# A hybrid decoder layer: the last gate summed at half the pace, weight sums in pairs, outputs of Down gated earlier, and an accumulator of its own for the last columns

## The chip, the cores and the metric

One core of a Trainium2 chip runs the whole layer in one launch. The metric is the device time of the core in microseconds; the time before is the median of three runs. All arithmetic is float32; the matmuls take each operand in two parts (a rounded high part and the rest), so that one product is three matmuls.

## The reference

For 512 tokens of width 1024 the layer computes a modulated norm, a mixture of two kinds of heads, and then a gated MLP. The change touches the MLP and the gate behind it alone:

```
h2 = rmsnorm(x, norm2_g[l]) * (1.0 + sc2) + sh2
u = causal_dwconv(h2 @ w_up[l], conv_w[l], conv_b[l])
a, v = jnp.split(u, 2, axis=-1)
x = x + gt2 * ((jax.nn.silu(a) * v) @ w_down[l])
```

`gt2` is the last sixth of `silu(c) @ w_ada + b_ada`, a vector of 1024. `w_up` is 1024 x 5632, `w_down` 2816 x 1024.

## The kernel before, in words

The order of the instructions on each engine is the order in which the program writes them. SP issues the plain loads and stores, POOL the accumulating ones, and a queue does not go past an instruction that waits.

**Up.** There are 44 steps (`st`), two for each of 22 column blocks of 128: one for the half `a`, one for the half `v`. `up_mm(st)` (L1713) issues 24 matmuls of 512 columns (three for each of 8 row blocks) into one accumulator. `next_parts` gets the weights of the step after: SP loads a block of 1 MB as `raw` (L206; two transfers, two buffers), ACT casts half of it to `whi` (L144) and DVE subtracts to get `wlo` (L145). `up_post` (L1723) applies the convolution and the SiLU on ACT and DVE, and POOL multiplies the halves and forms sums and differences of the two halves of the tokens (L1738 to L1746); `put_by` (L1748) stores one set of them, `later`, in HBM.

**The gate.** `ada_last` (L1468) computes `gt2` for two halves of 512 columns. For each of 8 row blocks SP loads 256 KB of `w_ada` into `aw` (L1478), POOL multiplies by the column `cs` and adds to an accumulator (L1479, L1480). An advance of the generator does one row block; then one advance splits the sum into `rhi` and `rlo` (ACT L144, DVE L145), and one sums over the partitions with two matmuls against ones (L1487, L1488). The Up loop advances it at every step from 3 on, so that 20 advances fill steps 3 to 22.

**Weight sums.** Down multiplies 2 x 2 blocks in a scheme with seven products, and needs four sums of blocks of `w_down`. `weight_sums` (L1693) makes them in HBM, by copies of SP and accumulating transfers of POOL, all of 256 KB, in six stages two steps apart, for each of 11 blocks `j`: copies (L1699, L1700), adds (L1691), a copy (L1705), an add, a copy (L1709), an add. A copy waits for the adds of the stage before it.

**Down.** There are 22 rounds (`u`) in two phases of 11. In the first, four products for two token blocks `i` fill eight accumulators; they are combined into the five tiles `m1, u2, u3, b12, c22` on ACT and DVE. In the second, three products fill six accumulators. `dn_load(u)` issues the loads three rounds ahead (in the second phase also the stored `later` block, L1777); `dn_split(u)` casts and subtracts one round ahead. `late` (L1894) multiplies a finished tile by the gate and adds `x1` (L1876, L1877) during the second phase: `c22`, which is stored, and `u3`. The last two rounds are run product by product, so that outputs end one by one: `dn_out` (L1910) takes three DVE instructions of 512 columns for each of four outputs (L1912 to L1914), `dn_last` (L1917) two for the rows of `u3` (L1919, L1920), the last of them in two halves of 256 columns that share one accumulator.

Of the kernel before, what the change touches and what calls it, by code (L numbers as in the profile page):

```python
# [19 lines left out]
P = 128  # L20
T = 512
# [32 lines left out]
EARLY = 6  # L54
ADAS = (3, 4, 2)
# [48 lines left out]
def hybrid_layer_kernel(ctx: ExitStack, tc: tile.TileContext, d: dict, out: bass.AP, dbg=None):  # L104
# [1581 lines left out]
    wt1, wt4 = (hbm.tile([NU, P, 512], F32, name=n) for n in ("wt1", "wt4"))  # L1686
    wt23 = hbm.tile([NU, P, 2, 512], F32, name="wt23")
    b_ = [[wd_view[:, r:NFF:2, 512 * c:512 * c + 512] for c in range(2)] for r in range(2)]

    def add(o, w):  # L1690
        gp.dma_start(o, w, accum_op=ALU.add)  # L1691

    def weight_sums(st):  # L1693
        for off, n in ((0, 0), (2, 1), (4, 2), (6, 3), (8, 4), (10, 5)):
            j, r = divmod(st - 3 - off, 3)
            if r or not 0 <= j < NU:
                continue
            if n == 0:
                sp.dma_start(wt23[j, :, 1], b_[1][1][:, j])  # L1699
                sp.dma_start(wt1[j], b_[0][1][:, j])  # L1700
            elif n == 1:
                add(wt23[j, :, 1], b_[0][1][:, j])
                add(wt1[j], b_[0][0][:, j])
            elif n == 2:
                sp.dma_start(wt23[j, :, 0], wt23[j, :, 1])  # L1705
            elif n == 3:
                add(wt23[j, :, 0], b_[0][0][:, j])
            elif n == 4:
                sp.dma_start(wt4[j], wt23[j, :, 0])  # L1709
            else:  # L1710
                add(wt4[j], b_[1][0][:, j])
# [43 lines left out]
    wraw, wsp = {}, {}  # L1755
    turn = [0]

    def a_split(u, a):
# [33 lines left out]
    def dn_split(u):  # L1792
# [49 lines left out]
    for st in range(3, nst):  # L1842
# [7 lines left out]
        next(ada2, None)  # L1850
# [43 lines left out]
    def late(u):  # L1894
        if u - NU in (3, 4):
            i = u - NU - 3
            gated(c22, right, i, 2, 512)
            sp.dma_start(out_view[:, 2 + i, 512:1024], c22[:, i])
        if u - NU in (5, 6):
            gated(u3, left, u - NU - 5, 2, 0)  # L1900

    for u in range(NU, n - 2):
        ahead_of(u)
        late(u)
# [3 lines left out]
    ahead_of(n - 2)  # L1908

    def dn_out(m, i, base, g, row, col):  # L1910
        t = TMP([P, T])
        ve.tensor_tensor(t, accs[m, i], base[:, i], ALU.add)  # L1912
        ve.tensor_tensor(t, t, g, ALU.mult)
        ve.tensor_tensor(t, t, x1[row][:, col:col + 512], ALU.add)  # L1914
        sp.dma_start(out_view[:, row, col:col + 512], t)

    def dn_last(i, row, c0, c1):  # L1917
        t = TMP([P, T])[:, 0:c1 - c0]
        ve.tensor_tensor(t, accs[4, i][:, c0:c1], left[:, c0:c1], ALU.mult)  # L1919
        ve.tensor_tensor(t, t, u3[:, i, c0:c1], ALU.add)  # L1920
        sp.dma_start(out_view[:, row, c0:c1], t)

    for m, base, g, col in ((2, m1, left, 0), (3, b12, right, 512)):
        for i in range(2):
            for u in (n - 2, n - 1):
                dn_mm(u, m, i)
            dn_out(m, i, base, g, i, col)
    for u in (n - 2, n - 1):
# [40 lines left out]
```

## Time and profile before

| | |
|---|---|
| median of three runs | 688.0 us (687.71 to 689.7) |
| the profiled execution | 690.0 us |
| its span, first to last instruction | 688.2 us |
| TensorE busy | 669.7 us (97%) |
| VectorE (DVE), ScalarE (ACT), GpSimd (POOL) busy | 500.0, 353.5, 199.6 us |
| mean granted TensorE clock | 0.991 |
| HBM read, written | 123.29 MB, 29.50 MB |

A row of the timeline is: start in us from the span's start, duration, engine, line, operation, tile written and tiles read, shape, and in brackets how long the engine had been idle before it and what ended that. Matmuls overlap, so their pace is read from start to start. A row of waits is: who waited for whom, total us, times, the longest. Durations of one kind are in ns.

### The profile page before, as it was taken

Reading aid. Unit: us, or ns where it says so; the run is one execution under the profiler, and the core shown is the slowest. Engines: PE = TensorE matmul, PEld = TensorE weight load, DVE = VectorE, ACT = ScalarE, POOL = GpSimd, SP = SyncE. Lnnn points to the kernel's source line nnn. Section 1 sums busy time; section 2 is a strip of 40 time slices with the busy share of each in tenths; the row PEclk is TensorE's granted clock in tenths of the full one; section 3 lists DMA queues with packets and bytes.
Section 4 is the critical chain, followed back from the end, with each engine's and each line's share of the span. In section 5 each row is a group of like instructions: output and inputs, shape, how many; then the busy total and the mean of one; then the engine's idle time right before and its main releaser. Section 6 shows DMA issues by size and latency. Waiting matters only on the chain.

```text
span 688.2 us, 11140 instructions
## 1 busy us (share of the span) xinstructions
PE 669.7 (97%) x4147; PEld 552.5 (80%) x4148; DVE 500.0 (73%) x964; ACT 353.5 (51%) x657; POOL 199.6 (29%) x211
## 2 busy tenths in 40 slices
PE   8999999999999999999999999979999999999995
PEld 4778898688888888888988888758888888888884
DVE  5778988978899878788556665845545558566987
ACT  5755337746777776255534443333443336454550
POOL 1006120000010101100079958986455346000000
PEclk9999999999999999999999999989999999999998
DMA  9936363566314135142268989999999846975562
GB/s 340 411 126 214 97 222 118 193 201 201 92 34 157 60 121 187 62 127 92 62 175 239 229 190 257 249 218 248 256 288 250 195 125 217 357 255 179 185 261 92
DMA packets 102876, 130.44 MB, mean 190 GB/s; under 512 B 7116, under 2 KB 68389, under 8 KB 102823
## 3 DMA queue, kind: packets, MB, share of 16 engines
q1 hardware_dynamic: 96055, 117.09, 51.4%
q0 software_dynamic: 6336, 11.54, 10.6%
q10 hardware_dynamic: 432, 1.12, 0.4%
q8 instruction: 32, 0.52, 0.3%
q14 instruction: 21, 0.17, 0.1%
HBM read 123.29 MB, written 29.50 MB: 222 GB/s over the span
## 4 chain that ended last, share of the span: by engine, by line
PE 75%; DVE 11%; ACT 5%; DMA 3%; POOL 3%; issue 1%; SPq 1%; ACTq 0%; POOLq 0%; DVEq 0%
PE u L150 10%; PE u L148 10%; PE u L149 10%; PE dn L149 5%; PE dn L148 5%; PE dn L150 5%; PE accq L657 3%; DMA aw<-in_w_ada 2%; PE oh L148 2%; PE oh L149 2%; PE oh L150 2%; PE oT L1126 2%; PE F L1097 2%; PE pT L148 2%; PE pT L149 2%; PE pT L150 2%
## 5 line engine op out<-in xcount | busy, mean ns | idle before, releaser
L145 DVE TENSOR_TENSOR wlo<-raw,whi 128x1024 fp32r<-128x1024 f32 (+1 forms) x67 | 92.8, 1386 | 94.5 <-ACT whi L144 94.3
L150 PE MATMUL u<-h2h,wlo 128*128 128x512 f32 (+1 forms) x360 | 138.0, 383 | 0.8 <-DVE wlo L145 0.8
L148 PE MATMUL u<-h2h,whi 128*128 128x512 f32 (+1 forms) x360 | 137.8, 383 | 0.0
L149 PE MATMUL u<-h2l,whi 128*128 128x512 f32 (+1 forms) x360 | 137.6, 382 | 0.0
L144 ACT CAST whi<-raw 128x1024 fp32r<-128x1024 f32 (+1 forms) x67 | 68.7, 1027 | 78.2 <-PE u L149 70.2
L150 PEld LDWEIGHTS u<-h2h,wlo 128*128 128x128 f32 x360 | 68.2, 190 | 15.1 <-DVE wlo L145 2.2
L149 PEld LDWEIGHTS u<-h2l,whi 128*128 128x128 f32 x360 | 68.4, 190 | 13.2
L148 PEld LDWEIGHTS u<-h2h,whi 128*128 128x128 f32 x360 | 68.4, 190 | 12.7
L349 POOL TENSOR_TENSOR hrs<-hrs,mhalf 128x4 f32<-128x4 f32 (+2 forms) x16 | 18.6, 1173 | 90.7 <-DVE hrs L348 88.7
L1733 ACT ACTIVATE y<-y 128x512 f32<-128x512 f32 x22 | 13.9, 632 | 55.1 <-DVE y L1730 55.0
L144 ACT CAST whi<-wd 128x1024 fp32r<-128x1024 f32 x20 | 21.0, 1052 | 40.5 <-PE dn L150 34.0
L1064 ACT ACTIVATE pt<-pt,mx 128x128 f32<-128x128 f32 (+3 forms) x64 | 36.0, 564 | 9.2 <-DVE mx L1048 8.1
L145 DVE TENSOR_TENSOR wlo<-wd,whi 128x1024 fp32r<-128x1024 f32 x20 | 25.6, 1278 | 19.7 <-ACT whi L144 19.4
L148 PE MATMUL pT<-hT,whi 128*128 128x512 f32 x96 | 38.3, 399 | 0.0
L149 PE MATMUL pT<-hT,whi 128*128 128x512 f32 x96 | 37.6, 391 | 0.0
L150 PE MATMUL pT<-hT,wlo 128*128 128x512 f32 x96 | 37.5, 391 | 0.0
L1691 POOL DMA_DIRECT2D wt<-in_w_down x44 | 36.8, 984 | 0.0
L1729 DVE SCALAR_TENSOR_TENSOR y<-u,cv,y 128x511 f32<-128x511 f32 x44 | 32.6, 741 | 2.9 <-ACT y L1728 2.9
L149 PE MATMUL dn<-wlo,as 128*128 128x512 f32 x88 | 34.4, 390 | 0.1
L148 PE MATMUL dn<-whi,as 128*128 128x512 f32 x88 | 34.2, 389 | 0.0
L150 PE MATMUL dn<-whi,as 128*128 128x512 f32 x88 | 34.2, 389 | 0.0
L1730 DVE SCALAR_TENSOR_TENSOR y<-u,cv,y 128x510 f32<-128x510 f32 x44 | 32.9, 749 | 1.6
(355 smaller groups left out, 1617.1 us busy)
## 6 DMA issues: line engine op xcount, KB each, us to landing
raw<-in_w_up SPq DMA_DIRECT2D x44, 512.0 KB, 6.0
aw<-in_w_ada SPq DMA_DIRECT2D x24, 512.0 KB, 3.9
wt<-in_w_down POOLq DMA_DIRECT2D x44, 256.0 KB, 7.0
ada<-in_ada_first SPq DMA_DIRECT2D x16, 512.0 KB, 8.1
raw<-in_w_in SPq DMA_DIRECT2D x7, 1024.0 KB, 5.0
wt<-in_w_down SPq DMA_DIRECT2D x22, 256.0 KB, 6.8
wt<-wt SPq DMA_DIRECT2D x22, 256.0 KB, 5.4
wd<-in_w_down SPq DMA_DIRECT2D x11, 512.0 KB, 4.4
```

The lines of the kernel that those rows point to most:

```text
L144: sc.copy(hi, src)
L145: (eng or ve).tensor_tensor(lo, src, f32(hi), ALU.subtract)
L148: pe.matmul(o, ah, bh, start=start, stop=False, skip_group_check=True)
L149: pe.matmul(o, ah, bl, start=False, stop=False, skip_group_check=True)
L150: pe.matmul(o, al, bh, start=False, stop=stop, skip_group_check=True)
L349: gp.tensor_tensor(o, o, mhalf[:, 0:n], ALU.pow)
L657: pe.matmul(accq[i], h[:, e, i * P:(i + 1) * P], w[:, f], start=(k + e + f == 0), stop=(e == 1 and k == KT - 1), skip_group_check=True)
L1064: sc.activation(pt[:, sl], pt[:, sl], AF.Exp, bias=mx[:, e:e + 1], scale=-1.0, accum_out=su[:, h % 2, e:e + 1])
L1691: gp.dma_start(o, w, accum_op=ALU.add)
L1729: ve.scalar_tensor_tensor(y[:, 1:], u[:, :T - 1], cv[:, 44 + c:45 + c], y[:, 1:], ALU.mult, ALU.add)
L1730: ve.scalar_tensor_tensor(y[:, 2:], u[:, :T - 2], cv[:, c:c + 1], y[:, 2:], ALU.mult, ALU.add)
L1733: sc.activation(y, y, AF.Silu)
```

## The change

1. The gate: the Up loop advances the generator at odd steps only, from step 3 to 41.
2. Weight sums: blocks `j` are taken in pairs (five pairs and a single one). The three sums that one pair needs lie in one tile `wt` of HBM, the fourth in `wt4`; each stage is one transfer for a pair (the first copies are two), so that a first add moves 1 MB. Stages start every six steps and stand two steps apart as before. POOL issues 18 adds where it issued 44, SP 24 copies where it issued 44. The products 6 and 7 of the first phase read their weights in the other order, to fit the new layout.
3. The second phase's first four `later` blocks are loaded (`back`) and split during rounds 5 to 9 of the first phase.
4. All of `c22, m1, u3, b12` get the gate and `x1` during the second phase; an output of the last rounds is then one multiplication by the gate and one addition.
5. The last 256 columns: the round before last is gated and added to `u3` early (`rest`). The weights of the last round's product 4 for those columns are multiplied by the gate and split again (`wgt`), and the product goes to an accumulator of its own, `dnt`; one addition to `rest` gives the output.

Cut to what is spoken of:

```diff
-    wt1, wt4 = (hbm.tile([NU, P, 512], F32, name=n) for n in ("wt1", "wt4"))
-    wt23 = hbm.tile([NU, P, 2, 512], F32, name="wt23")
+    groups = [range(j, min(j + 2, NU)) for j in range(0, NU, 2)]
+    wt = [hbm.tile([len(js), P, 3, 512], F32, name=f"wt{g}") for g, js in enumerate(groups)]
+    wt4 = [hbm.tile([len(js), P, 512], F32, name=f"wt4_{g}") for g, js in enumerate(groups)]
...
-            j, r = divmod(st - 3 - off, 3)
-            if r or not 0 <= j < NU:
+            g, r = divmod(st - 3 - off, 6)
+            if r or not 0 <= g < len(groups):
                 continue
+            js = groups[g]
+            rows = slice(2 * js[0], 2 * js[-1] + 2)
+            even, odd = (wd_view[:, rows][:, r::2] for r in range(2))
+            t, t4 = wt[g].rearrange("j p a c -> p j a c"), wt4[g].rearrange("j p c -> p j c")
             if n == 0:
-                sp.dma_start(wt23[j, :, 1], b_[1][1][:, j])
-                sp.dma_start(wt1[j], b_[0][1][:, j])
+                sp.dma_start(t[:, :, 0], even[:, :, 512:])
+                sp.dma_start(t[:, :, 1], odd[:, :, 512:])
             elif n == 1:
-                add(wt23[j, :, 1], b_[0][1][:, j])
-                add(wt1[j], b_[0][0][:, j])
+                gp.dma_start(t[:, :, 0:2], even.rearrange("p j (a c) -> p j a c", a=2), accum_op=ALU.add)
             elif n == 2:
-                sp.dma_start(wt23[j, :, 0], wt23[j, :, 1])
+                sp.dma_start(t[:, :, 2], t[:, :, 1])
             elif n == 3:
-                add(wt23[j, :, 0], b_[0][0][:, j])
+                gp.dma_start(t[:, :, 2], even[:, :, 0:512], accum_op=ALU.add)
...
         put_by(st - 4)
-        next(ada2, None)
+        if st % 2:
+            next(ada2, None)
...
         ahead_of(u)
+        if 0 <= u - EARLY + 1 < PRE:
+            back(u - EARLY + 1)
+        if 0 <= u - EARLY < PRE:
+            a_split(u - EARLY + NU, PB.pop(u - EARLY))
...
+    def late(v):
+        for t, i in [bases.pop(0) for _ in range((0, 1, 2, 2, 1, 1, 1, 0, 0)[v])]:
+            g, row, col = home[id(t)]
+            gated(t, g, i, row, col)
+            if t is c22:
+                sp.dma_start(out_view[:, row + i, col:col + 512], t[:, i])
...
+    def out_sum_of(acc, base, g):
+        t = TMP([P, T])[:, 0:acc.shape[1]]
+        ve.tensor_tensor(t, acc, g, ALU.mult)
+        ve.tensor_tensor(t, t, base, ALU.add)
+        return t
...
+    wgt = TMP([P, T], tag="wgt")[:, 0:256]
+    ve.tensor_tensor(wgt, w4raw[:, 256:512], left[:, 256:512], ALU.mult)
+    wgh, wgl = (G([256], F32R, s="wgt") for _ in range(2))
+    split(wgh, wgl, wgt)
+    both(2, 0)
+    dn_out(2, 0, m1, left, 0, 0)
...
+    dn_mm(n - 2, 4, 1)
+    rest = out_sum_of(accs[4, 1][:, 256:512], u3[:, 1, 256:512], left[:, 256:512])
...
+    dn_mm(n - 1, 4, 1, slice(0, 256))
+    dn_out(4, 1, u3, left, 3, 0, 256)
+    tail = PS("dnt")[:, 0:256]
+    ah, al = (z[:, P:2 * P] for z in AS[n - 1][TERMS[1][4][0]])
+    mm3(tail, ah, al, wgh, wgl, True, True)
+    t = TMP([P, T])[:, 0:256]
+    ve.tensor_tensor(t, tail, rest, ALU.add)
+    sp.dma_start(out_view[:, 3, 256:512], t)
```

How it moves instructions, at three places. First POOL in Up, before, from an add of weights on (`wt` the sums, `aw` the gate, `ga` and `gb` the products of the halves):

```order
L1691 DMA wt_3799<-in_w_down 128x512
L1691 DMA wt_3797<-in_w_down 128x512
L1479 TENSOR_TENSOR aw_4288<-aw_4288,cs 128x512
L1480 TENSOR_TENSOR aw_4288<-aw_4288 128x512
L1691 DMA wt_3799<-in_w_down 128x512
L1738 TENSOR_TENSOR gb_4453<-y_4496,y_4539 128x512
L1739 TENSOR_TENSOR ga_4452<-gb_4453 128x256
L1740 TENSOR_TENSOR ga_4452<-ga_4452 128x256
L1741 TENSOR_TENSOR gb_4453<-gb_4453,ga_4452 128x256
L1479 TENSOR_TENSOR aw_4288<-aw_4288,cs 128x512
L1480 TENSOR_TENSOR aw_4288<-aw_4288 128x512
L1479 TENSOR_TENSOR aw_4288<-aw_4288,cs 128x512
```

The same engine now, around the first add of the second pair:

```order
L1739 TENSOR_TENSOR gb_4453<-y_4494,y_4534 128x512
L1740 TENSOR_TENSOR ga_4452<-gb_4453 128x256
L1741 TENSOR_TENSOR ga_4452<-ga_4452 128x256
L1742 TENSOR_TENSOR gb_4453<-gb_4453,ga_4452 128x256
L1480 TENSOR_TENSOR aw_4297<-aw_4297,cs 128x512
L1481 TENSOR_TENSOR aw_4297<-aw_4297 128x512
L1704 DMA wt_3798<-in_w_down 128x2x1024
L1745 TENSOR_TENSOR ga_4617<-y_4574,y_4613 128x256
L1746 TENSOR_TENSOR gb_4618<-y_4574,y_4613 128x256
```

Between two sets of products stand one pair of gate instructions and one transfer; before, two pairs and one to three transfers.

Second SP in Up, before (`raw` is the next weights of Up):

```order
L206 DMA raw_4508<-in_w_up 128x8x128 x2
L1478 DMA aw_4288<-in_w_ada 128x512
L1705 DMA wt_3799<-wt_3799 128x512
L1478 DMA aw_4288<-in_w_ada 128x512
L1709 DMA wt_3798<-wt_3799 128x512
L206 DMA raw_4592<-in_w_up 128x8x128 x2
```

And now:

```order
L207 DMA raw_4503<-in_w_up 128x8x128 x2
L1479 DMA aw_4297<-in_w_ada 128x512
L1710 DMA wt_0_3803<-wt_3797 128x2x512
L207 DMA raw_4582<-in_w_up 128x8x128 x2
L1752 DMA later<-gb_4453 128x768
L1479 DMA aw_4297<-in_w_ada 128x512
L1706 DMA wt_3798<-wt_3798 128x2x512
L207 DMA raw_4667<-in_w_up 128x8x128 x2
```

A copy of a sum, which waits for an add, now stands right ahead of each load of Up's weights but every third, where two copies of 512 KB stand that wait for none.

Third the last instructions of DVE, before (`dn` are accumulators, `dc` the five tiles, `gt` the gate):

```order
L1912 TENSOR_TENSOR tmp_6834<-dn_6479,dc_6413 128x512
L1913 TENSOR_TENSOR tmp_6834<-tmp_6834,gt_3800 128x512
L1914 TENSOR_TENSOR tmp_6834<-tmp_6834,x_648_3499 128x512
L1919 TENSOR_TENSOR tmp_6845<-dn_6483,gt_3800 128x512
L1920 TENSOR_TENSOR tmp_6845<-tmp_6845,dc_6412 128x512
L1919 TENSOR_TENSOR tmp_6855<-dn_6487,gt_3800 128x256
L1920 TENSOR_TENSOR tmp_6855<-tmp_6855,dc_6412 128x256
L1919 TENSOR_TENSOR tmp_6862<-dn_6487,gt_3800 128x256
L1920 TENSOR_TENSOR tmp_6862<-tmp_6862,dc_6412 128x256
```

And now:

```order
L1927 TENSOR_TENSOR tmp_6798<-tmp_6798,dc_6390 128x512
L1926 TENSOR_TENSOR tmp_6805<-dn_6458,gt_3809 128x256
L1927 TENSOR_TENSOR tmp_6805<-tmp_6805,dc_6389 128x256
L1926 TENSOR_TENSOR tmp_6814<-dn_6450,gt_3809 128x512
L1927 TENSOR_TENSOR tmp_6814<-tmp_6814,dc_6390 128x512
L1926 TENSOR_TENSOR tmp_6824<-dn_6454,gt_3809 128x512
L1927 TENSOR_TENSOR tmp_6824<-tmp_6824,dc_6389 128x512
L1926 TENSOR_TENSOR tmp_6831<-dn_6458,gt_3809 128x256
L1927 TENSOR_TENSOR tmp_6831<-tmp_6831,dc_6389 128x256
L1960 TENSOR_TENSOR tmp_6839<-dnt_6835,tmp_6805 128x256
```

One addition stands behind the last product (`dnt`); `rest` (tmp_6805) has moved ahead of two outputs, and ahead of these rows stand the product and the subtraction of `wgt`.

More of the change, by code (lines that the diff above doesn't have):

```diff
@@ L54 @@
 EARLY = 6
+PRE = 4
 ADAS = (3, 4, 2)
@@ L1753, in put_by @@
                 a_split(j, PA.pop(j))
-    wraw, wsp = {}, {}
+    wraw, wsp, w4s = {}, {}, []
     turn = [0]
@@ L1762, in a_split, with back @@
         AS[u] = [(hi[:, q], lo[:, q]) for q in range(n)]
+    def back(j):
+        PB[j] = G([3, 256], s="gb")
+        sp.dma_start(PB[j], later[j])
     def dn_load(u):
@@ L1892, in hybrid_layer_kernel @@
                 ve.tensor_tensor(c22[:, i], o, u3[:, i], ALU.subtract)
[L1894 to L1900, printed above, removed]
+    bases = [(c22, 0), (c22, 1), (m1, 0), (m1, 1), (u3, 0), (u3, 1), (b12, 0), (b12, 1)]
+    home = {id(m1): (left, 0, 0), id(b12): (right, 0, 512), id(u3): (left, 2, 0), id(c22): (right, 2, 512)}
+    def late(v):
[4 more added lines that the diff above has]
+                sp.dma_start(out_view[:, row + i, col:col + 512], t[:, i])
     for u in range(NU, n - 2):
         ahead_of(u)
-        late(u)
+        late(u - NU)
         for m in TERMS[1]:
@@ L1908, in hybrid_layer_kernel @@
     ahead_of(n - 2)
[L1910 to L1928, printed above, removed]
-        dn_mm(u, 4, 0)
-    dn_last(0, 2, 0, 512)
-    dn_mm(n - 2, 4, 1)
-    for c in range(0, 512, 256):
-        dn_mm(n - 1, 4, 1, slice(c, c + 256))
-        dn_last(1, 3, c, c + 256)
+    w4raw = w4s[0][:, 0]
+    def out_sum_of(acc, base, g):
[3 more added lines that the diff above has]
+        return t
@@ new lines, in dn_out, with both @@
+    def dn_out(m, i, base, g, row, col, c1=512):
+        t = out_sum_of(accs[m, i][:, 0:c1], base[:, i, 0:c1], g[:, 0:c1])
+        sp.dma_start(out_view[:, row, col:col + c1], t)
+    def both(m, i):
+        for u in (n - 2, n - 1):
+            dn_mm(u, m, i)
+    wgt = TMP([P, T], tag="wgt")[:, 0:256]
[4 more added lines that the diff above has]
+    dn_out(2, 0, m1, left, 0, 0)
@@ new lines, in hybrid_layer_kernel @@
+    both(2, 1)
+    dn_out(2, 1, m1, left, 1, 0)
+    both(3, 0)
+    dn_out(3, 0, b12, right, 0, 512)
+    dn_mm(n - 2, 4, 1)
+    rest = out_sum_of(accs[4, 1][:, 256:512], u3[:, 1, 256:512], left[:, 256:512])
+    both(3, 1)
+    dn_out(3, 1, b12, right, 1, 512)
+    both(4, 0)
+    dn_out(4, 0, u3, left, 2, 0)
+    dn_mm(n - 1, 4, 1, slice(0, 256))
[3 more added lines that the diff above has]
+    mm3(tail, ah, al, wgh, wgl, True, True)
```

22 lines of the change are left out of this document (10 added, 12 removed).

## The prediction

> **What bounds the kernel now.** I read the page's first line and its busy times, then the stretches, then what PE waits for, and then the timeline where PE stood idle.
>
> ```profile
> span 688.2 us, 11140 instructions
> PE 669.7 (97%) x4147; PEld 552.5 (80%) x4148; DVE 500.0 (73%) x964; ACT 353.5 (51%) x657; POOL 199.6 (29%) x211
> ```
>
> TensorE is the bound: it is busy for all but 18.5 us. A gain here is an idle time of PE that goes, nothing else. Four stretches (PE, PEld, DVE, ACT, POOL busy with instructions, then granted clock, DMA share, GB/s):
>
> ```profile
> 360.00:400.00 40.00, 40.00 (x178) 33.10 (x177) 26.07 (x25) 17.27 (x22) 36.73 (x32) 1.00 0.89 220
> ...
> 440.00:480.00 40.00, 34.38 (x135) 26.81 (x135) 22.36 (x22) 13.97 (x18) 30.89 (x30) 0.91 1.00 238
> 480.00:520.00 40.00, 40.00 (x178) 33.14 (x177) 20.93 (x24) 15.56 (x19) 19.58 (x23) 1.00 1.08 271
> ```
>
> Up runs without a hole but for the second row. POOL, with a helper's work, is 92% busy before it. The waits name the hole and the one other that matters (total, times, longest):
>
> ```profile
> ACT rhi L144 <- POOL aw L1480: 13.9, 2, 9.8
> ...
> PE dn L148 <- DVE tmp L1919: 3.6, 1, 3.6
> PE ps L1487 <- ACT rhi L144: 3.4, 1, 3.4
> ```
>
> PE's timeline through the hole:
>
> ```profile
> 441.01 0.50 PE L150 MATMUL u<-h2h,wlo 128*128 128x512 f32 x1 [0.79 <-DVE wlo L145]
> ...
> 451.50 0.39 PE L150 MATMUL u<-h2h,wlo 128*128 128x512 f32 x1
> 455.24 0.50 PE L1487 MATMUL ps<-rhi,onesr 128*128 128x512 f32 x1 [3.36 <-ACT rhi L144]
> 457.21 0.80 PE L1488 MATMUL ps<-rlo,onesr 128*128 128x512 f32 x1 [1.46 <-DVE rlo L145]
> 457.80 0.63 PE L148 MATMUL u<-h2h,whi 128*128 128x512 f32 x1
> ...
> 463.64 0.40 PE L149 MATMUL u<-h2l,whi 128*128 128x512 f32 x1
> 463.87 0.39 PE L150 MATMUL u<-h2h,wlo 128*128 128x512 f32 x1
> ```
>
> A matmul of 512 columns starts every 0.227 us (463.64 to 463.87). From 451.50 to 463.64 lie 16 starts, worth 3.6 us; they took 12.1. So the hole costs 8.5 us, of which 2.9 is a slow clock: 13 starts from 457.80 on took 5.84 us instead of 2.95.
>
> ```profile
> 456.00:463.60 7.60, 6.38 (x14) 4.60 (x15) 5.39 (x6) 4.06 (x7) 6.41 (x7) 0.55 0.92 163
> ```
>
> Behind it stands POOL, which finishes the gate's last sum late and holds ACT for 9.8 us, and so the cast of Up's next weights too:
>
> ```profile
> 448.13 1.04 POOL L1479 TENSOR_TENSOR aw<-aw,cs 128x512 f32<-128x512 f32 x1 [1.00 <-DMA aw<-in_w_ada]
> ...
> 453.28 1.26 POOL L1480 TENSOR_TENSOR aw<-aw 128x512 f32<-128x512 f32 x1
> ```
>
> **The change part by part.** The sum is made against the profiled execution: 690.0 us, span 688.2 and 1.8 around it. The median of the runs is 688.0, 2.0 lower; I come back to that.
>
> *The gate at every second step.* A step of Up is 24 starts, 5.44 us. The generator has 20 advances; they now fill steps 3 to 41 where they filled 3 to 22. Per two steps POOL loses one of two multiply-and-add pairs and some issues of accumulating transfers:
>
> ```profile
> L1479 POOL TENSOR_TENSOR aw<-aw,cs x16: 1030/1042/2022, 350.9 to 451.6; 128x512 f32<-128x512 f32 x16
> L1480 POOL TENSOR_TENSOR aw<-aw x16: 1260/1292/2323, 352.1 to 453.3; 128x512 f32<-128x512 f32 x16
> ```
>
> ```profile
> L1691 POOL DMA_DIRECT2D wt<-in_w_down x44 | 36.8, 984 | 0.0
> ```
>
> POOL was busy 10.0 of 10.9 us in two steps (36.73 of 40). One pair is 2.3 us by the medians. The 44 issues of 0.98 us become 18; over about 40 steps that is 2.2 per two steps down to 0.9, 1.3 us less. It leaves some 6.4 of 10.9. The second half, at 5.3 of 10.9 (19.58 of 40), gets the pair and comes to about 7. The split of a sum now stands two steps behind its last add, and the matmul two further steps behind the split, 10.9 us each. So the matmuls on PE find their operand ready, and ACT waits for POOL only if POOL is over 10 us late. I take the whole hole, 8.5 us, and the 0.8 at 441.01, a weight split that came late in the same congestion: 9.3 us. What is late next is the weights of Up, which hang on SP.
>
> *Weight sums in pairs.* The bytes are the same; a first add is now 1 MB in one transfer, where four of 256 KB stood. The copy two steps (10.9 us) later waits for it at SP's head, and right behind that copy stand the next Up weights, the gate's load and the store of `later`. No such add is in the trace, so it is bounded.
>
> ```profile
> q0 software_dynamic: 6336, 11.54, 10.6%
> ```
>
> ```profile
> raw<-in_w_up SPq DMA_DIRECT2D x44, 512.0 KB, 6.0
> ...
> wt<-in_w_down POOLq DMA_DIRECT2D x44, 256.0 KB, 7.0
> ```
>
> ```profile
> SPq L1705 <- DMA wt<-in_w_down: 45.8, 8, 7.7
> ```
>
> The queue of the adds took 10.6% of 688 us, 73 us of all 16 engines, for 11.54 MB: 6.6 us for 1 MB if nothing else ran. Four landings of 7.0 us one after the other are 28 us. With the engines shared about evenly I take 13 us, twice the lower end, since the DMA share is near 1. That holds SP some 2 to 3 us, less than the 7.7 it already stood at that very copy. What covers it:
>
> ```profile
> 511.98 2.00 SPq L206 DMA_DIRECT2D raw<-in_w_up x2
> ```
>
> ```profile
> 525.95 1.05 ACT L144 CAST whi<-raw 128x1024 fp32r<-128x1024 f32 x1 [0.80 <-PE u L149]
> ```
>
> ```profile
> 531.42 0.39 PE L148 MATMUL u<-h2h,whi 128*128 128x512 f32 x1
> ```
>
> A load issued at 511.98 is cast at 525.95 and wanted on PE at about 531.4, 19.4 us after. It needs about 6.0 us to land and 2.3 for cast and subtraction, so SP may come 11 us late before PE waits. Hence nothing for this part, with an upper end of 17 us of SP's lateness (28 less 10.9), 6 us of PE's waiting at each of five groups; a gain beyond the stalls already counted is excluded, since PE has no other idle time in Up. The Trainium skill, in "DMA: Bandwidth & Descriptors", section "Anatomy of one DMA — SWDGE (gpsimd) path", prices such a transfer at about 2.0 us plus its bytes over 436 GB/s, an estimated 4.4 us for 1 MB; by that the copy would never wait and the rivals on transfers below would have next to no chance. Its figure for 256 KB would be 2.6 us where this trace has 7.0, so the measurement decides and they keep their chance.
>
> *Down: earlier loads, earlier splits, gating inside the second phase.* Four `later` blocks are loaded and split during the first phase (0.95 us of DVE in each of four steps with about 1.9 us of DVE idle). Four more gated outputs, two DVE instructions each, move from the end into the second phase.
>
> ```profile
> 636.70 0.95 DVE L145 TENSOR_TENSOR as<-gb,as 128x768 fp32r<-128x768 f32 x1
> 637.57 1.22 DVE L145 TENSOR_TENSOR wlo<-wd,whi 128x1024 fp32r<-128x1024 f32 x1
> ...
> 639.31 0.95 DVE L145 TENSOR_TENSOR as<-gb,as 128x768 fp32r<-128x768 f32 x1
> ...
> 648.69 0.69 DVE L1876 TENSOR_TENSOR dc<-dc,gt 128x512 f32<-128x512 f32 x1
> ...
> 650.02 0.95 DVE L145 TENSOR_TENSOR as<-gb,as 128x768 fp32r<-128x768 f32 x1
> ```
>
> ```profile
> 639.09 0.39 PE L149 MATMUL dn<-wlo,as 128*128 128x512 f32 x1
> ```
>
> A step of DVE's splits is 2.6 us (636.70 to 639.31), 1.7 where the `as` split is done already; a gated output is 1.33 (648.69 to 650.02); a step of PE is 18 starts, 4.08 us. The tightest place now is 637.57: that `wlo` ends 0.3 us before PE wants it at 639.09. Its `as` split goes, so it starts at 636.70. Then the steps carry 1, 2, 2, 1, 1, 1 outputs: DVE is free at 641.9, 647.3, 652.5, 656.5, and the next `wlo` ends at 654.6 against PE's want of 655.4, then 658.6 against 659.5. Nothing waits, with 0.8 us to spare at the least: nothing, 0 to 2 us as the upper end, and no gain, as PE had no wait there.
>
> *The end.* Here DVE is last.
>
> ```profile
> 673.47 0.69 DVE L1912 TENSOR_TENSOR tmp<-dn,dc 128x512 f32<-128x512 f32 x1 [0.22 <-PE dn L150]
> ...
> 681.69 0.68 DVE L1919 TENSOR_TENSOR tmp<-dn,gt 128x512 f32<-128x512 f32 x1
> ...
> 683.02 0.42 DVE L1919 TENSOR_TENSOR tmp<-dn,gt 128x256 f32<-128x256 f32 x1
> ...
> 685.00 0.42 DVE L1920 TENSOR_TENSOR tmp<-tmp,dc 128x256 f32<-128x256 f32 x1
> ```
>
> Before: four outputs of three instructions (8.2 us), one of two (1.33), then halves with a 3.6 us wait of PE for DVE's reading of the shared accumulator; done at 685.42. After: about 673.2 the gated weights, 0.42, a cast on ACT of about 0.5 (estimated below the 0.61 that the 512-wide ones take) and 0.42, so DVE begins the outputs at about 674.5; five at 1.33, two halves at 0.84, one last add at 0.42: 683.3. PE is ahead throughout (its last starts would come near 680). That is 2.1 us; between 1 (if the cast waits longer) and 2.6.
>
> Sum: 690.0 - 9.3 - 2.1 = 678.6. If the 2.0 us between profile and median are part of the hole, that holds for the median too; if they lie elsewhere, 676.6. I take 677.6.
>
> **The rivals.**
> - *Transfers become the bound*: Up's traffic, evened out, is 8.7 MB in six steps (16 sums of 0.262 MB, three weight blocks of 1.05, one and a half `later`, three gate blocks), 267 GB/s, close to the 271 that the row 480 to 520 delivered at a DMA share of 1.08. For it: no reserve. Against: PE did not wait in that row, and the first half asked for about 290. PE would wait 1 to 5 us in all: 678.6 to 682.6. Chance 0.17.
> - *Slower*: the 1 MB add takes over 24 us (10.9 + 11 + 2.3). From there each of five groups stops PE for over 2.3 us and the 11.4 us are gone; at 25.5 us it is 3.6 us each, 18 us: 696.6. For it: 28 is the bound from single landings. Against: those landings overlapped others. The Trainium skill, in "TensorE: Matmul & The Clock Gate", Part 1, says that PE falls to half clock after an idle window of about 3.4 us; the one hole here agrees (clock 0.55), and by that rule such stalls would each cost nearly 3 us more, an estimated 711. Chance 0.04.
> - *The hole moves*: POOL still ends a sum late, by waiting for a gate load behind SP's blocked copy, and ACT stands at the split as it did for 9.8 us. Half the hole stays: 682 to 686. Against: 10.9 us of distance. Chance 0.05.
> - *DVE late in the second phase*: 1 to 2 us: 679.6. Chance 0.04.
> - *The end gives nothing* (a wait of DVE for the cast, or for the shared accumulator): 679.7. Chance 0.04.
>
> **How the numbers follow.** My forecast has 0.66; its own range is 675.5 to 679.5. The range that holds 8 in 10 takes in the transfers and the two small ones: 674.5 to 683.0. No change means within 0.3%, 2.1 us of 688.0, about what a measurement of this kernel can tell. Slower: 0.04; same: 0.03, the worst of the moved hole; faster: 0.93.
>
> **What would show it.** Right: no wait of PE for `rhi` or `rlo`, a clock of 1.00 throughout Up, POOL near 60 to 65% busy in Up, SP standing a few us at the copy behind the 1 MB add, the last DVE instruction about 2 us sooner after PE's first output of the end. Wrong: waits of PE for `wlo` in Up at every sixth step (transfers), ACT idle at `rhi`, PE waiting for `wlo` or `as` between the starts of the second phase, or a gap of DVE before its first output that is longer than the cast.

## The result, and the profile after

| | before | after |
|---|---|---|
| median of four runs | 687.86 us (687.48 to 689.7) | 678.34 us (677.88 to 678.53) |
| the profiled execution, its span | 690.0, 688.2 | 678.53, 676.7 |
| granted clock | 0.991 | 0.999 |

The ratio is 0.9855, with a 95% interval of 0.9837 to 0.9874: faster by 9.5 us in the medians. The profile after, its first line and the busy times:

```profile
span 676.7 us, 11052 instructions
...
PE 665.1 (98%) x4147; PEld 550.6 (81%) x4148; DVE 497.8 (74%) x971; ACT 354.3 (52%) x658; POOL 183.5 (27%) x185
```

TensorE now stands idle for 11.6 us of the span where it stood for 18.5. The stretches (PE, PEld, DVE, ACT, POOL busy with instructions, then granted clock, DMA share, GB/s):

```profile
360.00:400.00 40.00, 40.00 (x178) 33.12 (x177) 23.36 (x26) 16.51 (x20) 23.15 (x21) 1.00 0.82 227
400.00:440.00 40.00, 40.00 (x178) 33.14 (x177) 24.64 (x24) 17.71 (x22) 30.80 (x26) 1.00 0.97 263
440.00:480.00 40.00, 40.00 (x178) 33.08 (x177) 23.06 (x24) 17.42 (x22) 23.56 (x23) 1.00 1.05 292
```

The second number of each row says it: PE has no gap left, and its clock is whole. POOL is busy for 23 to 31 us of 40 where the first of these stretches had 36.73. The third row also shows that the transfers were not at a limit before: 292 GB/s where the best such stretch of Up before had 271. In the list of what PE waits for, the longest is now a wait from the kernel's beginning, which was there before too; no wait for `rhi`, for a part of Up's weights or for the shared accumulator is among them:

```profile
PE warm L339 <- DVE sel L528: 1.6, 1, 1.6
```

The gate has two pairs of matmuls, one for each half of its columns. Before, the second pair, at 455.24, stood 3.4 and 1.5 us; the first pair, at 395.59, had passed without a wait. Now the second pair comes at 554.07 and passes at PE's own pace of 0.227 us (the first pair, at 444.79, does too):

```profile
554.07 0.39 PE L1488 MATMUL ps<-rhi,onesr 128*128 128x512 f32 x1
554.30 0.39 PE L1489 MATMUL ps<-rlo,onesr 128*128 128x512 f32 x1
554.53 0.40 PE L149 MATMUL u<-h2h,whi 128*128 128x512 f32 x1
```

To see how much came from Up and how much from the end, I look for one matmul that both kernels have: the first of the last product by product round. In the timeline of PE before:

```profile
671.50 0.39 PE L148 MATMUL dn<-whi,as 128*128 128x512 f32 x1
```

And after:

```profile
661.99 0.39 PE L149 MATMUL dn<-whi,as 128*128 128x512 f32 x1
```

So 9.5 us had come by then. The rest of DVE's timeline after:

```profile
663.66 0.42 DVE L1939 TENSOR_TENSOR wgt<-wd,gt 128x256 f32<-128x256 f32 x1
664.55 0.42 DVE L146 TENSOR_TENSOR wgt<-wgt,wgt 128x256 fp32r<-128x256 f32 x1 [0.47 <-ACT wgt L145]
664.90 0.68 DVE L1926 TENSOR_TENSOR tmp<-dn,gt 128x512 f32<-128x512 f32 x1
...
673.12 0.42 DVE L1960 TENSOR_TENSOR tmp<-dnt,tmp 128x256 f32<-128x256 f32 x1
```

From that matmul to DVE's last end are 11.55 us (661.99 to 673.54), where before had 13.92 (671.50 to 685.42): 2.4 us from the end. The last store takes 0.4 us more to the span's end, which makes the 11.5 us between the two spans.

### The profile page after: what moved, and what is told of

Same layout as the page of the kernel before. It is cut to its first block, busy times and chain, and to the rows that moved or that the text cites. A ratio compares the mean times of both kernels' runs of the same rounds, so it can differ in the third digit from the quotient of the medians.

```text
span 676.7 us, 11052 instructions
## 1 busy us (share of the span) xinstructions
PE 665.1 (98%) x4147; PEld 550.6 (81%) x4148; DVE 497.8 (74%) x971; ACT 354.3 (52%) x658; POOL 183.5 (27%) x185
## 3 DMA queue, kind: packets, MB, share of 16 engines
q0 software_dynamic: 4512, 11.54, 9.5%
## 4 chain that ended last, share of the span: by engine, by line
PE 81%; DVE 10%; ACT 5%; DMA 2%; issue 1%; ACTq 0%; SPq 0%; DVEq 0%
PE u L150 12%; PE u L149 12%; PE u L151 12%; PE dn L149 5%; PE dn L150 5%; PE dn L151 5%; PE accq L658 3%; PE oh L149 2%; PE oh L151 2%; PE oh L150 2%; PE oT L1127 2%; PE F L1098 2%; PE pT L149 2%; PE pT L151 2%; PE pT L150 2%
## 5 line engine op out<-in xcount | busy, mean ns | idle before, releaser
L146 DVE TENSOR_TENSOR wlo<-raw,whi 128x1024 fp32r<-128x1024 f32 (+1 forms) x67 | 90.9, 1358 | 100.5 <-ACT whi L145 100.4
L1729 ACT ACTIVATE y<-u,cv 128x512 f32<-128x512 f32 x44 | 34.0, 773 | 0.0
## 6 DMA issues: line engine op xcount, KB each, us to landing
wt<-in_w_down POOLq DMA_DIRECT2D x5, 1024.0 KB, 11.7
```

Source lines behind the costliest of these rows:

```text
L146: (eng or ve).tensor_tensor(lo, src, f32(hi), ALU.subtract)
L1729: sc.activation(y, u, AF.Identity, bias=cv[:, 132 + c:133 + c], scale=cv[:, 88 + c:89 + c])
```

## The experiments

Each ratio is to runs of the kernel before that were taken beside the kernel in question.

| run | edit | median us (range) | ratio to the kernel before, 95% |
|---|---|---|---|
| e1_gate_half | before, gate at every second step | 683.75 (680.94 to 684.6) | 0.9923 (0.9904 to 0.9942) |
| e2_sums_pairs | before, sums in pairs | 692.04 (688.68 to 694.81) | 1.0052 (1.0035 to 1.007) |
| e3_end | before, parts 3 to 5 | 686.47 (685.6 to 691.32) | 0.9981 (0.9963 to 0.9999) |
| e4_gate_dve | before, gate's sums on DVE | 683.44 (680.54 to 686.57) | 0.993 (0.9905 to 0.9955) |
| e5_after_old_sums | after, sums not in pairs | 680.21 (677.32 to 682.43) | 0.987 (0.9835 to 0.9905) |
| e6_groups4 | after, sums in fours | 678.27 (677.71 to 679.64) | 0.985 (0.9815 to 0.9884) |
| e7_pairs_far | e2, copies a step further behind the first add | 688.05 (685.83 to 692.21) | 0.9996 (0.9972 to 1.0019) |
| e8_end_pool | after, gated weights on POOL | 677.41 (677.32 to 679.18) | 0.9839 (0.9811 to 0.9867) |
| a_again | after, once more | 678.71 (678.37 to 680.02) | 0.9849 (0.9833 to 0.9866) |
| e9_end_shared | after, shared accumulator | 678.17 (677.49 to 679.9) | 0.9844 (0.9826 to 0.9861) |
| e10_end_pool2 | e8, one addition on POOL | 678.17 (677.83 to 678.49) | 0.9838 (0.9823 to 0.9852) |
| e11_gate_each | after, gate at every step | 689.91 (688.11 to 693.33) | 1.0027 (1.0005 to 1.005) |

**The gate's pace, alone and undone.** My theory: POOL with the gate at every step is the cause of the hole. The rival: something else in Up is late, and the hole moves. First the gate's pace alone, put into the kernel before:

```diff
-        next(ada2, None)
+        if st % 2:
+            next(ada2, None)
```

> The kernel before with the gate alone at every second step of Up; weight sums, Down and the end as before. Theory POOL (the hole came because POOL, 92% busy, ended the gate's sum late): the hole goes whole, PE waits for neither rhi nor rlo, the time is that of the changed kernel plus the 2.3 us of the end, 680.0 to 681.0 us. Rival transfers (the hole came because the first half of Up asked for about 290 GB/s): the same here, since the gate's loads are spread too. Rival sums (the many small transfers and their issues were the cause): a part of the hole stays, 683 us or more.

Measured 683.75, above what the theory expected; two of the six runs, at 680.94 and 681.38, came near it. The time is the third rival's, its mechanism is not: the hole at the gate's matmuls was gone whole. But the weights of Up came late at two places, with 2.9 us of idle time in all. This is the first of them, followed 1.3 us later by a wait of 0.53 us for `wlo`:

```profile
511.33 0.50 PE L148 MATMUL u<-h2h,whi 128*128 128x512 f32 x1 [1.04 <-ACT whi L144]
```

Behind it, in SP's and POOL's timelines, stands a copy of the sums: POOL issued the adds at 491.74, SP waited at the copy until 501.45, and the load of Up's weights behind it went out at 502.02. So the gate's pace alone is worth 4.4 us in the medians, and part of the gain hangs on something else. Then the changed kernel with the gate alone undone:

```diff
-        if st % 2:
-            next(ada2, None)
+        next(ada2, None)
```

> The changed kernel with only the gate undone: its generator advances at every step again, the weight sums stay in pairs, the end stays new. Theory (the gate's pace is the lever; pairs with the gate at every step make SP stand behind adds that POOL issues late): the hole of the run with the pairs alone comes back, near 455 to 467 us, with stalls at the weights before it; 692.0 less the 1.7 to 2.4 of the end: 689 to 691, POOL near 80% busy from 360 to 440. Rival (pairs and the new end carry the gain, the gate little): 679 to 681.

Measured 689.91, within the theory's range and slightly slower than before the change (the interval of the ratio begins at 1.0005): without the gate's pace the other parts, taken together, bring nothing. In it the hole can be followed from link to link. SP first, whose queue holds the copy of the sums (L1706), Up's weights (L207) and the gate's loads (L1479):

```profile
425.70 2.30 SPq L1479 DMA_DIRECT2D aw<-in_w_ada  x2
438.16 0.55 SPq L1706 DMA_DIRECT2D wt<-wt  x1
...
442.26 1.09 SPq L1479 DMA_DIRECT2D aw<-in_w_ada  x2
```

After two gate loads at 425.70, SP came to the copy at about 428.0 and stood there for 10 us, because it waits for the add before it, and this is when POOL issued that add:

```profile
427.33 1.16 POOL L1704 DMA_DIRECT2D wt<-in_w_down  x1
...
450.30 1.04 POOL L1480 TENSOR_TENSOR aw<-aw,cs 128x512 f32<-128x512 f32 x1 [7.20 <-DMA aw<-in_w_ada]
...
453.76 1.26 POOL L1481 TENSOR_TENSOR aw<-aw 128x512 f32<-128x512 f32 x1
```

The program puts the copy two steps, 10.9 us, behind the add; POOL was so late that less than 1 us was left of them. Its lateness can be reckoned from PE, which ran without a stall here and began step 13 at 396.22:

```profile
396.22 0.40 PE L149 MATMUL u<-h2h,whi 128*128 128x512 f32 x1
```

The add belongs to step 17, four steps of 5.44 us later, at 418.0; POOL issued it 9.4 us after that. The copy belongs to step 19, at 428.9, and SP was on time for it. The gate's loads behind the copy went out at 442.26, so POOL in its turn stood idle for 7.2 us at 450.30 and finished the sum at 455.0. Then ACT (9.5 us of waiting) and PE:

```profile
ACT rhi L145 <- POOL aw L1481: 13.9, 2, 9.5
```

```profile
455.72 0.80 PE L1488 MATMUL ps<-rhi,onesr 128*128 128x512 f32 x1 [4.20 <-ACT rhi L145]
458.04 0.80 PE L1489 MATMUL ps<-rlo,onesr 128*128 128x512 f32 x1 [1.52 <-DVE rlo L146]
```

POOL and SP hold each other: POOL late, its add late, SP at the copy, the gate's load late, POOL later still.

**Less work or more distance?** At half the pace POOL has less to do in a step, and the split of a sum also stands twice as far behind its last addition. To look at these apart, POOL gets less work at the old distance: the gate at every step as before, its product and sum in one instruction on DVE, one step after the load.

```diff
-                raw = aw[:, k % 2]
-                sp.dma_start(raw, ada_view[:, k, c0:c0 + 512])
-                gp.tensor_tensor(raw, raw, cs[:, k:k + 1].to_broadcast([P, 512]), ALU.mult)
-                gp.tensor_tensor(acc, acc, raw, ALU.add)
+                sp.dma_start(aw[:, k % 2], ada_view[:, k, c0:c0 + 512])
+                if k:
+                    ve.scalar_tensor_tensor(acc, aw[:, (k - 1) % 2], cs[:, k - 1:k], acc, ALU.mult, ALU.add)
...
+            ve.scalar_tensor_tensor(acc, aw[:, 1], cs[:, KT - 1:KT], acc, ALU.mult, ALU.add)
```

> The kernel before with the gate at every step as before, but its multiply and add in one instruction of DVE, one step after the load, in place of two of POOL. The gate's loads keep their pace, so the first half of Up asks for the same 290 GB/s; only POOL is relieved. Theory POOL: the hole goes, 680 to 681.5 us; POOL about 60% busy in the first half. Rival transfers: the hole, or several small ones where PE waits for wlo, stays: 685 to 689 us.

Measured 683.44, between the theory's range and the rival's. PE no longer waits for `rhi` at all, with the gate's loads at their old pace and the split at its old distance. So it takes POOL to make the hole; neither the transfers nor the distance make it by themselves. But the edit also takes POOL off the path to `rhi`, so it doesn't tell how much less work on POOL would have been enough, nor how much the longer distance adds; that stays open. What is left is a stall of another kind, on PE:

```profile
426.71 0.80 PE L150 MATMUL u<-h2h,wlo 128*128 128x512 f32 x1 [2.75 <-DVE wlo L145]
```

DVE was late with `wlo` because it now carries the wait for the gate's load itself, and `wlo` stands behind it:

```profile
424.77 0.75 DVE L1479 SCALAR_TENSOR_TENSOR aw<-aw,cs 128x512 f32<-128x512 f32 x1 [5.55 <-DMA aw<-in_w_ada]
425.43 1.22 DVE L145 TENSOR_TENSOR wlo<-raw,whi 128x1024 fp32r<-128x1024 f32 x1
```

It cost less than the hole (PE was idle for 2.7 us of the 40 from 400 on, where the hole took 5.6 of the 40 from 440 on), and it shows where a wait must not stand: ahead of work that PE wants.

**The pairs.** Part 2 of the change alone, with the new layout that Down reads:

```diff
-            j, r = divmod(st - 3 - off, 3)
+            g, r = divmod(st - 3 - off, 6)
...
-                add(wt23[j, :, 1], b_[0][1][:, j])
-                add(wt1[j], b_[0][0][:, j])
+                gp.dma_start(t[:, :, 0:2], even.rearrange("p j (a c) -> p j a c", a=2), accum_op=ALU.add)
```

> The kernel before with the weight sums in pairs alone; the gate at every step, Down and the end as before. Theory POOL: POOL's load falls from 10.0 to about 8.7 of 10.9 us in two steps, so the hole shrinks and may stay in part: 682 to 687 us. Rival transfers: as many bytes in the first half, so the hole stays, 686 to 689 us, or worse. Rival sums: the hole goes whole, 680 to 681 us.

Measured 692.04, slower than before by 3.9 us, where the theory had expected a gain. The hole stayed, and PE stood a second time, some 10 us earlier, for the weights:

```profile
447.39 0.50 PE L148 MATMUL u<-h2h,whi 128*128 128x512 f32 x1 [2.44 <-ACT whi L144]
...
458.82 0.50 PE L1487 MATMUL ps<-rhi,onesr 128*128 128x512 f32 x1 [3.26 <-ACT rhi L144]
461.13 0.80 PE L1488 MATMUL ps<-rlo,onesr 128*128 128x512 f32 x1 [1.81 <-DVE rlo L145]
```

An add of 1 MB takes longer to land than one of 256 KB (medians of 11.1 us in this run and 7.0 us in the kernel before), and where POOL is late all of that is SP's standing. To test this link, the copy behind the 1 MB add and all stages after it were put a step further back (the very last add stays where it was). Against the run of the pairs alone:

```diff
-        for off, n in ((0, 0), (2, 1), (4, 2), (6, 3), (8, 4), (10, 5)):
+        for off, n in ((0, 0), (2, 1), (5, 2), (7, 3), (9, 4), (11, 5)):
-            g, r = divmod(st - 3 - off, 6)
+            g, r = divmod(st - 3 - off + (n == 5 and st == nst - 1), 6)
```

> The kernel before with the weight sums in pairs (as in the run of that edit alone), but the copy behind the 1 MB add stands three steps behind it instead of two, and what follows one step later too (the very last add stays where it was). In the run of the edit alone SP stood 10.6 us at that copy behind an add that POOL had issued 9.7 us late; the gate's loads behind it came late, POOL waited 8.6 us for them and TensorE stood. Theory (SP's standing at that copy is a link of the loop): SP's waits for the adds fall from 88 us to under 50, the late gate load goes, and the hole of 12 us shrinks or goes: 680 to 687. Rival (POOL's load alone makes the hole, SP only follows): the hole stays where it was, 690 to 693.

Measured 688.05, 4.0 us below the pairs alone (the intervals of the two ratios lie apart), between the theory's range and the rival's, and the same as the kernel before. SP's waits at this copy fell from 49.4 us to one of 2.1; what remains of the 88 us is the second copy, where they rose from 38.6:

```profile
SPq L1709 <- DMA wt<-in_w_down: 46.8, 6, 11.1
```

PE's waits at the gate fell from 3.3 and 1.8 us to these; no wait for `whi` is left, and two of 0.7 us at most for `wlo`:

```profile
PE ps L1487 <- ACT rhi L144: 2.7, 1, 2.7
...
PE ps L1488 <- DVE rlo L145: 0.6, 1, 0.6
```

So SP's standing is a link of the loop, as the theory said: with it shortened the hole shrinks. That it stays fits POOL's own load as the other link; this run does not show that by itself.

Next the changed kernel with the pairs undone, that is, single blocks with the gate at half its pace and the new end (one stage of it shown):

```diff
-                gp.dma_start(t[:, :, 0:2], even.rearrange("p j (a c) -> p j a c", a=2), accum_op=ALU.add)
+                add(wt23[j, :, 1], b_[0][1][:, j])
+                add(wt1[j], b_[0][0][:, j])
```

> The changed kernel with one edit undone: the weight sums go back to single blocks of 256 KB (the gate stays at every second step, the end stays new). Theory: POOL and SP hold each other in a loop (POOL late, its adding transfers issued late, SP stands at the copy behind them, Up weights and gate loads late, POOL later still); halving the gate breaks the loop for the most part and the pairs take out the rest, which in the kernel with the halved gate alone was 3.4 us of stalls at 511, 512 and 552 us. Then this kernel is about 2 us (the end) below that one's 683.75: 681 to 682.5, with short waits of TensorE for the parts of Up weights. Rival 1: the pairs give nothing once the gate is halved (the 3.4 us were chance): 678 to 679, like the changed kernel. Rival 2: the pairs cost something by themselves (alone they made the kernel 3.9 us slower): 676 to 677.5.

Measured 680.21, between the theory's range and that of the first rival. Its profiled execution had one stall in Up:

```profile
PE u L151 <- DVE wlo L146: 1.5, 1, 1.5
```

The median is 1.5 to 1.9 us above the changed kernel's two medians, but the intervals of the ratios overlap. What the pairs bring on top of the halved gate is therefore not settled; the runs spread from 677.3 to 682.4 without them and from 677.9 to 680.0 with them.

Last, the other way: sums in fours, whose first add is 2 MB.

```diff
-    groups = [range(j, min(j + 2, NU)) for j in range(0, NU, 2)]
+    groups = [range(j, min(j + 4, NU)) for j in range(0, NU, 4)]
...
-            g, r = divmod(st - 3 - off, 6)
+            g, r = divmod(st - 3 - off, 12)
```

> The changed kernel with the weight sums in groups of four blocks: the first add is 2 MB in one transfer (the others 1 MB), twice the changed kernel's, issued every 12 steps; the distance from an add to the copy behind it stays two steps (10.9 us). Theory: 1 MB landed in 8.4 to 12.7 us, so 2 MB land in 17 to 25; SP stands at the copy 6 to 14 us beyond its time, and more where POOL issues late; the cover is 11 us, so TensorE waits a few us in Up once or twice: 680 to 686. Rival 1 (the cover is larger than worked out, or the loads run ahead): 678 to 679, with SP's wait at the copy near 15 us and no wait of TensorE. Rival 2 (the slower case of the prediction: from an add over 24 us on, every group stops TensorE, at a slow clock): 2 or 3 stalls of 5 to 10 us, 688 or more.

Measured 678.27, as the first rival said. The add did not take twice as long as one of 1 MB. Sizes and median landing times of the adds in this run:

```profile
wt<-in_w_down POOLq DMA_DIRECT2D x2, 2048.0 KB, 13.6
...
wt<-in_w_down POOLq DMA_DIRECT2D x4, 1024.0 KB, 11.8
```

SP stood as long as the rival said, 15.9 us at the longest, and PE did not wait. The first group shows the cover; SP's rows, and ACT's first cast behind them:

```profile
350.11 1.81 SPq L1479 DMA_DIRECT2D aw<-in_w_ada  x1
366.90 0.56 SPq L1706 DMA_DIRECT2D wt<-wt  x1
367.57 1.19 SPq L207 DMA_DIRECT2D raw<-in_w_up  x2
```

```profile
373.92 1.05 ACT L145 CAST whi<-raw 128x1024 fp32r<-128x1024 f32 x1 [0.78 <-DMA raw<-in_w_up]
...
379.22 1.06 ACT L145 CAST whi<-raw 128x1024 fp32r<-128x1024 f32 x1 [3.57 <-PE u L150]
```

After 15 us of standing the load went out at 367.57 and was cast at 373.92, only 0.8 us later than ACT was ready for it; the next cast waits for PE again. Standing is not lateness: DVE's last reading of the `raw` buffer that this load fills ended at 359.9, so for the first 8 of those 15 us SP would have waited in any case, and the load was some 7.6 us late, below the 11 of cover.

**The end.** Parts 3, 4 and 5 of the change alone, in the kernel before (the loads and splits of `later` ahead, four more outputs gated during the second phase, the own accumulator):

```diff
-    def dn_out(m, i, base, g, row, col):
-        t = TMP([P, T])
-        ve.tensor_tensor(t, accs[m, i], base[:, i], ALU.add)
-        ve.tensor_tensor(t, t, g, ALU.mult)
-        ve.tensor_tensor(t, t, x1[row][:, col:col + 512], ALU.add)
+    def out_sum_of(acc, base, g):
+        t = TMP([P, T])[:, 0:acc.shape[1]]
+        ve.tensor_tensor(t, acc, g, ALU.mult)
+        ve.tensor_tensor(t, t, base, ALU.add)
```

> The kernel before with the parts on Down alone: four blocks loaded and split early, all outputs gated in the second phase, two instructions for an output, an accumulator of its own for the last columns. The hole in Up stays. All theories: 2.0 to 2.4 us less, 685.5 to 686.0 us. If the hole swallows or hands on some of it, 687 us or more.

Measured 686.47 against 688.13 beside it, 1.7 us in the medians, a little less than expected. Its trace has the gain whole: from the first matmul of the last round, at 669.14, to DVE's last end, at 680.69, are 11.55 us, where before had 13.92. Which part of the new end is it? The changed kernel was run once more, beside two variants of its end:

> The changed kernel once more, word for word, beside the next two kernels on the same chip, since they are to be told from it by less than 1 us: 677.9 to 678.6 as in its first runs.

Measured 678.71, 0.1 above the range expected. Its trace has 11.54 us from that matmul to DVE's last end (663.49 to 675.03), so this distance repeats to 0.01 us over three executions with the new end.

The first variant puts the last 256 columns back into the shared accumulator:

```diff
-    wgt = TMP([P, T], tag="wgt")[:, 0:256]
-    ve.tensor_tensor(wgt, w4raw[:, 256:512], left[:, 256:512], ALU.mult)
-    wgh, wgl = (G([256], F32R, s="wgt") for _ in range(2))
-    split(wgh, wgl, wgt)
...
-    rest = out_sum_of(accs[4, 1][:, 256:512], u3[:, 1, 256:512], left[:, 256:512])
...
-    mm3(tail, ah, al, wgh, wgl, True, True)
-    t = TMP([P, T])[:, 0:256]
-    ve.tensor_tensor(t, tail, rest, ALU.add)
+    dn_mm(n - 1, 4, 1, slice(256, 512))
+    t = out_sum_of(accs[4, 1][:, 256:512], u3[:, 1, 256:512], left[:, 256:512])
```

> The changed kernel without its own accumulator of the last piece and the gated weights for it: the last 256 columns go into the shared accumulator's second half as before, and TensorE waits there for DVE's reading of the first half; the outputs gated beforehand stay. Theory (DVE paces the end; the gated weights cost DVE 1.24 us before the first output, from 663.66 to 664.90, and the wait of TensorE for the shared accumulator is hidden behind DVE's lateness for the most part): outputs begin at 663.7, five of 1.33 end at 670.3, and from there the kernel before took 2.40 us to its last instruction: 672.7 where the changed kernel has 673.54, so 677.4 to 677.7, a little faster than the changed kernel. Rival (the own accumulator is what the end gains from): the wait of TensorE comes back at 2 us or more, 679.5 to 680.5.

Measured 678.17 against 678.71. PE does wait for the shared accumulator again, and its first matmul of the last round is quoted for the count:

```profile
661.08 0.39 PE L149 MATMUL dn<-whi,as 128*128 128x512 f32 x1
...
671.01 0.38 PE L149 MATMUL dn<-wg,as 128*128 128x256 f32 x1 [1.49 <-DVE tmp L1925]
```

```profile
672.12 0.43 DVE L1926 TENSOR_TENSOR tmp<-tmp,dc 128x256 f32<-128x256 f32 x1
```

From 661.08 to 672.55 are 11.47 us, against 11.55 with the own accumulator: the same. The own accumulator takes PE's wait away and puts the gated weights in front of DVE's first output; the two cancel. The theory had expected 0.8 us less, since it had not counted that the outputs come to stand behind PE as soon as DVE begins earlier. So beside the gated weights on DVE the own accumulator gains nothing, and the gain of the end is that of the outputs gated beforehand, with the early loads and splits that make room for them.

The gated weights need not be DVE's work. The same product and subtraction on POOL, one round earlier:

```diff
+    w4raw = wraw[n - 1][1][:, 0]
+    wgt = TMP([P, T], tag="wgt")[:, 0:256]
+    gp.tensor_tensor(wgt, w4raw[:, 256:512], left[:, 256:512], ALU.mult)
+    wgh, wgl = (G([256], F32R, s="wgt") for _ in range(2))
+    split(wgh, wgl, wgt, gp)
     ahead_of(n - 2)
```

> The changed kernel, but the gated weights for the own accumulator of the last piece (their product with the gate and the subtraction that splits it) are made on the idle POOL, one unit earlier, instead of on DVE between the last weight split and the first output. Theory (DVE is last at the end: outputs begin when the split of the gated weights is through, and DVE ended 3.0 us behind TensorE's last matmul start): DVE begins the first output 0.8 to 1.0 us sooner and all behind it with it: 677.2 to 677.6, until the outputs wait for TensorE, which needs 1.36 us for each against DVE's 1.33. Rival: TensorE paces the outputs already, so that only the first moves: 678.2 to 678.5.

Measured 677.41, the lowest median of all kernels here. Its first matmul of the last round:

```profile
661.57 0.39 PE L149 MATMUL dn<-whi,as 128*128 128x512 f32 x1
```

And DVE's outputs, the first of which now waits for PE:

```profile
663.60 0.69 DVE L1930 TENSOR_TENSOR tmp<-dn,gt 128x512 f32<-128x512 f32 x1 [0.22 <-PE dn L151]
...
671.57 0.42 DVE L1931 TENSOR_TENSOR tmp<-tmp,dc 128x256 f32<-128x256 f32 x1
671.91 0.42 DVE L1960 TENSOR_TENSOR tmp<-dnt,tmp 128x256 f32<-128x256 f32 x1
```

From 661.57 to 672.33 are 10.76 us, 0.8 less than the changed kernel's 11.55, as expected. The ratios' intervals do not separate the two kernels; the traces do. It is also 0.7 less than the 11.47 with the shared accumulator: the own accumulator pays once DVE is not the one to pay for it.

One more step the same way, the last addition of output (4, 0) on POOL as well:

```diff
-    dn_out(4, 0, u3, left, 2, 0)
+    dn_out(4, 0, u3, left, 2, 0, 512, gp)
```

> The kernel with the gated weights on POOL, and in addition the last addition of output (4, 0) on POOL instead of DVE. There TensorE paces all outputs up to that one (read 0.1 us after its last matmul), and DVE still does three more instructions behind its multiplication. Theory: the addition, 0.61 us of DVE's time, runs on POOL beside the two last pieces; 0.4 to 0.6 us less than 677.4, so 676.8 to 677.0. Rival: POOL's addition of 128x512 takes 1.3 us or more and its store becomes the last: 677.4 or a little more.

Measured 678.17: no gain, as the rival said of the time, but not for its reason. POOL's addition took 1.26 us and its store was not the last. DVE's row and POOL's say why:

```profile
671.15 1.25 DVE L1931 TENSOR_TENSOR tmp<-tmp,dc 128x256 f32<-128x256 f32 x1
```

```profile
670.86 1.26 POOL L1931 TENSOR_TENSOR tmp<-tmp,dc 128x512 f32<-128x512 f32 x1 [11.46 <-DVE tmp L1930]
```

Beside POOL's addition DVE's of 256 columns took 1.25 us where it took 0.42 without: what DVE was spared it lost again. From the first matmul of the last round, at 661.86, to DVE's last end are 10.88 us, against 10.76.

## Why the prediction was right, point by point

The time lay 0.7 us above the forecast of 677.6, inside the range.

- **The hole, 9.3 us: right in the sum, in part by luck.** The last round began 9.5 us earlier. The prediction put all of it down to the gate's pace, which does not bring it alone (next point); that nothing was left in the changed kernel hangs on parts that it had priced at nothing or had not seen together. That POOL is behind it was shown by the changed kernel with the gate undone (689.91) and by the gate's sums on DVE (no wait for `rhi`).
- **That this hangs on the gate's pace alone: wrong.** By itself it brought 4.4 us; undone in the changed kernel it cost 11.2 to 11.6. The parts don't add up, and the prediction had priced them one by one; the traces of the two runs, where POOL and SP hold each other, show the way in which one part's lateness becomes another's. Its sentence that the weights of Up are what is late next was right, and in the run of the gate's pace alone they were late.
- **POOL at 60 to 65%: right in the mean**, 64% from 360 to 560; single stretches of 40 us had 58 to 77%.
- **The 1 MB add, 13 us: nearly right**, 11.7. The adds of 512 KB and 1 MB in the changed kernel, with their median landing times:

```profile
wt<-in_w_down POOLq DMA_DIRECT2D x11, 512.0 KB, 8.6
...
wt<-in_w_down POOLq DMA_DIRECT2D x5, 1024.0 KB, 11.7
```

- **The pairs at nothing: right beside the halved gate, as far as the runs can tell, for the cover that was named.** The 11 us of cover held with adds of 2 MB too, so the slower rival's 24 us were far away. That pairs cost 3.9 us where POOL runs late was missing from the prediction: it let the copy stand two steps behind the add, and in the traces with the gate at every step POOL's lateness had used up these two steps.
- **SP standing 2 to 3 us at the copy: wrong.** It stood 10.4 us at the longest:

```profile
SPq L1706 <- DMA wt<-in_w_down: 46.6, 6, 10.4
```

Here POOL was not late. It issued this add, of step 11, as PE began that step:

```profile
384.95 0.39 PE L149 MATMUL u<-h2h,whi 128*128 128x512 f32 x1
```

```profile
384.86 1.17 POOL L1704 DMA_DIRECT2D wt<-in_w_down  x1
```

```profile
386.23 0.42 SPq L1479 DMA_DIRECT2D aw<-in_w_ada  x1
397.09 0.55 SPq L1706 DMA_DIRECT2D wt<-wt  x1
```

It was SP that was early: it came to the copy at 386.65, and PE began the copy's step, 13, only at 395.8 (two steps of 5.44 us after 384.95). The prediction had SP arrive with PE's steps. Standing of this kind cost nothing; the load behind the copy went out at 397.74, and PE did not wait.

- **Transfers as the bound: did not come.** 292 GB/s in the busiest of Up's stretches above, and PE without a wait.
- **The second phase of Down, nothing: right**, no wait of PE between its starts.
- **The end, 2.1 us: right in size (2.4), half right in cause.** DVE began the outputs 2.9 us after the round's start (3.0 predicted). But the own accumulator, counted as a part of it, is worth nothing as long as DVE makes its gated weights.
- **The step from the profile to the median: mis-sized.** The profiled execution before was 2.0 us above its median, and I put half of that into the forecast. The sum against the profiled execution was 678.6 and the median after is 678.34: all of the 2.0 us went. That fits waits of the kind that the change removed, but only one execution of the kernel before has a trace, so it is not shown. Before, 23 runs beside the first experiments spread from 686.3 to 692.3; after, the eight runs spread from 677.9 to 680.0.

## What to carry to other kernels

When two in-order queues wait for each other's work, price an edit by the lateness that is there, not by the distance that the program writes: with the gate at every step, a copy two steps behind an add had under 1 us left of 10.9. But look at which of the two is off its time: a queue that stands because it came early costs nothing. The parts of such a change don't add up, so undo each one in the finished kernel as well as trying it alone. Before work is moved to an idle engine at the end, ask which engine runs beside it at that moment.

## What the runs showed of the hardware

- An accumulating transfer from HBM to HBM takes long even when it is small, and grows much less than its size: medians of 7.0 (44 transfers), 8.6 (11), 11.7 (5) and 13.6 us (2) for 256 KB (kernel before), 512 KB, 1 MB (changed kernel) and 2 MB (sums in fours), all beside these kernels' other traffic. The upper end of my bound, four landings of 256 KB one after the other, was more than twice what 1 MB took. The Trainium skill, in "DMA: Bandwidth & Descriptors", section "Anatomy of one DMA — SWDGE (gpsimd) path", has a constant part and one for the bytes too; by its figures 2 MB would be an estimated 6.8 us. The form agrees roughly with these rows, the height does not, and the measurement decides.
- An addition of 128x256 on DVE, begun beside a running one on POOL, took 1.25 us, and 0.42 without. The Trainium skill, in "SBUF — State Buffer", section "Who interferes with whom", says that a DVE instruction with two inputs in SBUF contends with one of POOL that reads SBUF, and that the order of issue decides which of two is blocked. The rows agree: DVE's began 0.29 us after POOL's and ended 0.28 us after it, while POOL's took 1.26 us, no longer than the median of 1.29 us that its additions of 128x512 had in the kernel before.
